# Own tiles for the gate one-hots, and two stage buffers instead of three, in a PEER trunk kernel

## The chip, the cores and the metric

The kernel runs on one core of a Trainium2 chip. A core has four compute engines that run side by side, each with its own instruction queue: TensorE (PE, matrix products), VectorE (DVE), ScalarE (ACT) and GpSimd (POOL). SyncE (SP) only issues transfers; ACT and POOL issue some as well. Engines wait for one another through semaphores. The metric is the device time of one execution in microseconds (us), as the median of several runs.

## The reference

One layer of a decoder trunk over 1024 tokens of width 1024: a mixer with three branches, then an expert network in which each token uses 128 of 16384 experts (8 heads, 16 each).

```python
x = x + hybrid_mixer(rms_norm(x, norm_mix), ...)        # stick-breaking, sparse and recurrent branch
x = x + peer_ffn(rms_norm(x, norm_ffn), w_q, sub_keys, u_tab, v_tab)
return rms_norm(x, norm_final)

# peer_ffn, for 128 tokens at a time
s = einsum("nhad,akd->nhak", (xc @ w_q).reshape(...), sub_keys)   # two sets of 128 keys
top_s, top_i = top_k(s, 16)                                       # then the 16 best of the 256 sums
eidx = first * 128 + second                                       # expert number
gate = softmax(best_s)
hpre = einsum("nd,nhkd->nhk", xc, u_tab[eidx])
act = gate * gelu(hpre)
out = einsum("nhk,nhkd->nd", act, v_tab[eidx])
```

## The kernel before

**Two ways for the experts.** The tokens are worked in four parts of 256 (`PARTS`). For parts 0 and 3 the chosen rows of `u_tab` and `v_tab` are gathered one by one: GpSimd issues an indirect transfer, VectorE multiplies or adds the row (`gather_tile`, L1145 to L1157, tiles `u`, `v`, `gacc`). Parts 1 and 2 (`DENSE`, 512 tokens) go through all 16384 experts: a loop over 128 blocks of 128 experts forms `g = u . h` (`gemm1`, L1386), applies the nonlinearity, multiplies by a gate that is zero for experts not chosen (`gt`, L1429), and sums `g . v` into PSUM (`gemm2`, L1434). This loop comes after the mixer and takes the last 1470 us; it is called the dense loop here. The gathers run beside everything from the first routing on.

**The gates of the dense parts.** The dense loop needs, per token, a 128 x 128 table of gates: row and column are the two halves of the expert number. The 128 choices of a token are scattered into that table by a matrix product of one-hots. `spread_pieces` (L1204) does it four tokens at a time, and a call of `four(q)` is one batch: L1215 compares the two index halves with 0 to 127 (one-hots `hs[:, 0:2]`), L1216 multiplies the second one-hot by the gate's high and low half (`hs[:, 2:4]`), eight matmuls (L1219, L1220) make the four tables in a PSUM tile `gb`, and ScalarE copies them to a staging buffer (L1222). Four batches fill a staging buffer with 16 tokens; then the ACT queue writes it to DRAM (L1224, 1 MB) into `d_G`. There are 128 batches and 32 groups, half of them for part 1 and half for part 2.

**Where these tiles live.** The one-hots are 4 KB per partition and come from the pool `w4` (`W4`, L103), four buffers taken in turn by many users: rows of `x`, norm weights, the routing's own one-hots, and, in the dense loop, the blocks of `u` (`uraw`, L1390). The staging buffers are three: two halves of `stages` (L293) and a tile `stage` of the pool `per`, chosen by `u = n0 // 16 % 3`. `stages` has the tag `h2`: its memory is given to the tile `h2` (L1382), the operand of the dense loop, when the mixer ends. `h2` is loaded from DRAM (`d_hx`, L1384) once the last transfer out of `stages` is done. The last two groups (`n0 >= TH - 32`) go to `stage`, as the group before them does.

**What sets the order.** The program text is written out by a planner (L1305 to L1379) that mixes the pieces of one part with those of others; spread pieces are fillers without a due time. Near the end of the mixer it alternates two spread pieces with one piece of the last part's tail: `merge` (the branch products `pb`, with L919 and L921), then `wo` (output projections `pj_wo`, with weights `w_wo` loaded by SP at L248). Then the framework orders each engine's instructions by priority, over a modelled run in which a tile is taken when a buffer of its pool is free; so the order on an engine may differ from the program's. [...] Projections and `gb` share the two PSUM buffers `ps_mm`.

Of the kernel before, what the change touches and what calls it, by code (L numbers as in the profile page):

```python
# [10 lines left out]
F32 = mybir.dt.float32  # L11
F16 = mybir.dt.float16
# [23 lines left out]
TH = 512  # L36
# [35 lines left out]
def trunk(ctx: ExitStack, tc: tile.TileContext, a: dict, out: bass.AP):  # L72
# [15 lines left out]
    per = mix.enter_context(tc.tile_pool(name="per", bufs=1))  # L88
# [14 lines left out]
    def W4(name, shape=(128, 1024), dt=F32):  # L103
        return w4.tile(list(shape), dt, tag="w4", name=name)
# [188 lines left out]
    stages = hpl.tile([128, 2, 128, 16], F32, tag="h2", name="stages", bufs=1)  # L293
# [910 lines left out]
    def spread_pieces(pt):  # L1204

        stage = {}

        def four(q):
            n0 = pt.t0 - TD + q * 4
            if q % 4 == 0:  # L1210
                u = n0 // 16 % 3 if n0 < TH - 32 else 2
                stage[0] = per.tile([128, 128, 16], F32, tag="stage", name=f"stage{n0}") if u == 2 else stages[:, u]
            sp = spread[pt.i][:, :, q * 4:q * 4 + 4]
            hs = W4(f"hot{n0}", (128, 4, 128, 4), F16)
            V.tensor_tensor(hs[:, 0:2], iorep.unsqueeze(1).to_broadcast([128, 2, 128, 4]), sp[:, 0:2].unsqueeze(2).to_broadcast([128, 2, 128, 4]), op=ALU.is_equal)  # L1215
            V.tensor_tensor(hs[:, 2:4], hs[:, 1:2].to_broadcast([128, 2, 128, 4]), sp[:, 2:4].unsqueeze(2).to_broadcast([128, 2, 128, 4]), op=ALU.mult)  # L1216
            ps = ps_mm.tile([128, 4, 128], F32, tag="mm", name=f"gb{n0}")
            for n in range(4):
                P.matmul(ps[:, n, :], hs[:, 0, :, n], hs[:, 2, :, n], start=True, stop=False)  # L1219
                P.matmul(ps[:, n, :], hs[:, 0, :, n], hs[:, 3, :, n], start=False, stop=True)  # L1220
            m0 = q % 4 * 4
            S.activation(stage[0][:, :, m0:m0 + 4].rearrange("p i n -> p n i"), ps, AF.Copy, scale=SA / SGT)  # L1222
            if q % 4 == 3:
                nc.scalar.dma_start(d_G[n0 // 16], stage[0])  # L1224

        return [lambda q=q: four(q) for q in range(pt.n // 4)]
# [338 lines left out]
```

## Time and profile before

| what | value |
|---|---|
| median of 3 runs | 3559.37 us (3555.66 to 3559.86) |
| the profiled execution | 3556.94 us, its span 3555.1 us |
| clock granted to TensorE, mean | 0.937 |
| L1215, one instruction | 0.683 us (median), 128 of them |
| L1216, one instruction | 0.683 us (median), 128 of them |
| L1222, one copy to a staging buffer | 1.067 us (median), 128 of them |
| first and last L1215 | 1190.5 and 2071.5 us |
| first matmul of the dense loop | 2083.30 us |

Times in the trace count from the start of the span. A row of the timeline gives the start, the length, the engine and line, the operation with output and inputs, and, in brackets, how long the engine stood idle before it and which instruction ended that idle time. `SPq` and `ACTq` are the issues of transfers on those queues. A row of the waits names who waited for whom, then the total, the number of times and the longest.

### The profile page before, as it was taken

What the parts mean: (1) busy time and instruction counts of PE and PEld (TensorE: products, weight loads), DVE (VectorE), ACT (ScalarE), POOL (GpSimd) and SP (SyncE); (2) the same over time, 40 slices, a digit from 0 to 9 for tenths busy, and PEclk for the clock granted to TensorE, in tenths of its full rate; (3) what the DMA queues carried; (4) which work ended last, traced back from release to release, by engine and by line L of the source; (5) the groups of instructions that cost most, each with busy time, mean ns of one, the idle gap of its engine ahead of it and who ended that gap; (6) DMA issues with size and microseconds to landing.
All of it is one profiled execution on the core that took longest, in us unless ns stands there. A gap on an engine that the chain in (4) does not pass through costs nothing.

```text
span 3555.1 us, 57087 instructions
## 1 busy us (share of the span) xinstructions
PE 3255.7 (92%) x20660; PEld 2181.6 (61%) x20660; DVE 3001.0 (84%) x6662; ACT 1599.9 (45%) x3162; POOL 1360.4 (38%) x1166
## 2 busy tenths in 40 slices
PE   7999899999997799999878879869999999999996
PEld 6887777777876587887666644434444444444443
DVE  5665669888789888888998868999988998989898
ACT  5776454653543465644356333234334333333332
POOL 0000001343332242223322234347764765766664
PEclk9999999999997799999778899989999999999998
DMA  8964865989977587897656799789998999999997
GB/s 303 322 240 150 279 206 197 327 314 311 360 284 239 170 307 253 307 331 277 219 190 214 278 353 332 242 267 372 388 375 314 375 381 351 371 352 380 342 373 260
DMA packets 359336, 1058.07 MB, mean 298 GB/s; under 512 B 35238, under 2 KB 107626, under 8 KB 354444
## 3 DMA queue, kind: packets, MB, share of 16 engines
q0 software_dynamic: 147456, 536.94, 42.1%
q1 hardware_dynamic: 206988, 483.93, 38.4%
q10 hardware_dynamic: 4608, 33.56, 2.4%
q8 instruction: 162, 2.65, 0.3%
q14 instruction: 122, 1.00, 0.1%
HBM read 944.19 MB, written 110.10 MB: 297 GB/s over the span
## 4 chain that ended last, share of the span: by engine, by line
PE 53%; DVE 23%; DMA 9%; issue 7%; ACT 6%; POOL 1%; SPq 0%; ACTq 0%; DVEq 0%; POOLq 0%
PE g L258 13%; PE acc L1436 10%; PE pj_mg L258 4%; DVE u L1147 4%; PE g L1436 3%; DVE gacc L1157 3%; PE pj_r_hg L258 2%; DMA v<-in_peer_v_dram,gidx 2%; PE pb L258 2%; DMA gt<-d_G 2%; DMA u<-in_peer_u_dram,gidx 2%; PE pj_wo L258 2%; PE gb L1219 1%; PE gb L1220 1%; PE z_sb L410 1%
## 5 line engine op out<-in xcount | busy, mean ns | idle before, releaser
L1155 POOL DMA_INDIRECT v<-in_peer_v_dram,gidx x421 | 553.6, 1315 | 689.8 <-DVE gacc L1157 410.1
L1145 POOL DMA_INDIRECT u<-in_peer_u_dram,gidx x417 | 523.5, 1255 | 636.8 <-DVE u L1147 404.9
L258 PE MATMUL g<-h,us 128*128 128x512 f16 x3072 | 690.8, 382 | 17.1 <-DVE ts L982 6.2
L1157 DVE SCALAR_TENSOR_TENSOR gacc<-v,act,gacc 128x1024 f32<-128x1024 f32 x421 | 538.1, 1278 | 35.4 <-DMA v<-in_peer_v_dram,gidx 31.8
L1436 PE MATMUL acc<-vs,ac 128*128 128x512 f16 x2304 | 536.8, 381 | 20.6 <-ACT vs L213 7.8
L1436 PEld LDWEIGHTS <-ac 128*128 128x128 f16 x3072 | 302.0, 98 | 411.4 <-issue 50.1
L258 PEld LDWEIGHTS <-us 128*128 128x128 f16 x3072 | 302.0, 98 | 385.1 <-issue 17.8
L1147 DVE SCALAR_TENSOR_TENSOR u<-u,gh 128x1024 f32<-128x1024 f32 x417 | 501.8, 1216 | 34.3 <-DMA u<-in_peer_u_dram,gidx 33.8
L1395 ACT ACTIVATE ge<-g 128x512 f32<-128x512 f32 x128 | 76.2, 595 | 528.7 <-PE g L258 498.4
L258 PE MATMUL pj_mg<-hT,w_mg 128*128 128x256 f16 x2304 | 273.9, 274 | 6.3 <-ACT mg L881 3.9
L258 PEld LDWEIGHTS <-w_mg 128*128 128x128 f16 x2304 | 226.8, 100 | 37.6 <-issue 11.8
L1436 PE MATMUL g<-vs,ac 128*128 128x512 f16 x768 | 184.0, 383 | 23.6 <-ACT ge L1395 23.6
L214 DVE SCALAR_TENSOR_TENSOR vs<-vraw,vs 128x1024 f16<-128x1024 f32 x128 | 154.8, 1215 | 25.9 <-ACT vs L213 25.8
L1145 POOL DMA_INDIRECT rr_u<-in_peer_u_dram,gidx x95 | 137.1, 1444 | 89.5 <-DVE rr_u L1147 66.3
L213 ACT ACTIVATE vs<-vraw 128x1024 f16<-128x1024 f32 x128 | 132.6, 1046 | 84.8 <-DMA vraw<-in_peer_v_dram 84.8
L213 ACT ACTIVATE ac<-ge 128x512 f16<-128x512 f32 x128 | 80.0, 628 | 200.7 <-DVE ge L1429 161.3
L1155 POOL DMA_INDIRECT rr_v<-in_peer_v_dram,gidx x90 | 130.7, 1453 | 94.3 <-DVE gacc L1157 71.5
L214 DVE SCALAR_TENSOR_TENSOR us<-uraw,us 128x1024 f16<-128x1024 f32 x128 | 155.6, 1215 | 9.8 <-ACT us L213 9.1
L258 PE MATMUL pb<-o,w_b 128*128 128x256 f16 x1152 | 144.8, 282 | 20.3 <-DVE sg L919 16.7
L1219 PE MATMUL gb<-hot 128*128 128x128 f16 x512 | 126.1, 294 | 39.2 <-DVE hot L1216 21.2
L258 PE MATMUL pj_r_hg<-hT,w_r_hg 128*128 128x256 f16 x1152 | 143.5, 283 | 7.1 <-ACT iv_hg L739 4.7
L1429 DVE TENSOR_TENSOR ge<-ge,gt 128x256 f32<-128x256 f32 x256 | 97.9, 419 | 55.7 <-ACT ge L1395 30.2
(1141 smaller groups left out, 6422.0 us busy)
## 6 DMA issues: line engine op xcount, KB each, us to landing
uraw<-in_peer_uT_dram SPq DMA_DIRECT2D x128, 512.0 KB, 7.2
vraw<-in_peer_v_dram SPq DMA_DIRECT2D x128, 512.0 KB, 8.1
w_mg<-dw SPq DMA_DIRECT2D x72, 512.0 KB, 5.0
gt<-d_G SPq DMA_DIRECT2D x32, 1024.0 KB, 18.5
d_G<-stages ACTq DMA_DIRECT2D x20, 1024.0 KB, 5.2
w_r_hg<-dw SPq DMA_DIRECT2D x36, 512.0 KB, 5.2
w_b<-dw SPq DMA_DIRECT2D x72, 256.0 KB, 5.0
wr_mg<-in_wblk_dram SPq DMA_DIRECT2D x24, 512.0 KB, 4.9
```

Source lines behind the costliest of these rows:

```text
L213: S.activation(hi, src, AF.Copy, scale=scale)
L214: V.scalar_tensor_tensor(lo, in0=src, scalar=scale, in1=hi, op0=ALU.mult, op1=ALU.subtract)
L258: P.matmul(ps, l[:, k, :], r[:, k, :], start=(i == 0), stop=(i == n - 1))
L410: P.matmul(x["z"], st["q"][b:b + 64, tl * 128:(tl + 1) * 128], st["k"][b:b + 64, r0 + c0:r0 + c1], start=True, stop=(c0 > 0))
L1145: G.indirect_dma_start(out=ur, out_offset=None, in_=a["peer_u"], in_offset=bass.IndirectOffsetOnAxis(ap=idx[:, c:c + 1], axis=0))
L1147: V.scalar_tensor_tensor(ur, in0=ur, scalar=1.0, in1=h2, op0=ALU.mult, op1=ALU.mult, accum_out=hpre[:, c:c + 1])
L1155: G.indirect_dma_start(out=vr, out_offset=None, in_=a["peer_v"], in_offset=bass.IndirectOffsetOnAxis(ap=idx[:, c:c + 1], axis=0))
L1157: V.scalar_tensor_tensor(acc, in0=vr, scalar=act[:, c:c + 1], in1=acc, op0=ALU.mult, op1=ALU.add)
L1219: P.matmul(ps[:, n, :], hs[:, 0, :, n], hs[:, 2, :, n], start=True, stop=False)
L1395: S.activation(ge, ps, AF.Gelu, scale=1.0 / (SW * SH2))
L1429: V.tensor_tensor(gv, gv, gt[:, :, i % 8, :], op=ALU.mult)
L1436: P.matmul(ps, ac[:, x, t * 128:(t + 1) * 128], v[:, y, dh * 512:(dh + 1) * 512], start=start and n == 0, stop=stop and n == 2)
```

## The change

The one-hots get a tag of their own with two buffers in the pool `per`, and leave `w4`. The tile `stage` goes; all 32 groups take turns in the two halves of `stages`, the last two included. The memory is the same: 8 KB per partition for `stage` before, two times 4 KB for `hot` now.

```diff
             if q % 4 == 0:
-                u = n0 // 16 % 3 if n0 < TH - 32 else 2
-                stage[0] = per.tile([128, 128, 16], F32, tag="stage", name=f"stage{n0}") if u == 2 else stages[:, u]
+                stage[0] = stages[:, n0 // 16 % 2]
             sp = spread[pt.i][:, :, q * 4:q * 4 + 4]
-            hs = W4(f"hot{n0}", (128, 4, 128, 4), F16)
+            hs = per.tile([128, 4, 128, 4], F16, tag="hot", name=f"hot{n0}", bufs=2)
```

## The prediction

> **What bounds the kernel now.** I read the page first (busy time, then the chain that ended last), then busy time by stretch, then the hand-over from the mixer to the dense expert loop row by row.
>
> ```profile
> span 3555.1 us, 57087 instructions
> PE 3255.7 (92%) x20660; PEld 2181.6 (61%) x20660; DVE 3001.0 (84%) x6662; ACT 1599.9 (45%) x3162; POOL 1360.4 (38%) x1166
> ...
> PE 53%; DVE 23%; DMA 9%; issue 7%; ACT 6%; POOL 1%; SPq 0%; ACTq 0%; DVEq 0%; POOLq 0%
> ```
>
> TensorE carries 53% of the chain and VectorE 23%, so a microsecond counts where PE stands idle. By stretch (start:end, length, then busy time and instructions of PE, PEld, DVE, ACT, POOL, then clock, DMA share, GB/s):
>
> ```profile
> 1790.00:2083.00 293.00, 235.57 (x1591) 189.07 (x1591) 244.60 (x438) 156.77 (x271) 85.97 (x73) 0.81 0.70 243
> 2083.00:2500.00 417.00, 367.54 (x1789) 181.30 (x1790) 376.80 (x879) 137.68 (x188) 200.65 (x145) 0.94 0.89 315
> 2500.00:3000.00 500.00, 500.00 (x2319) 226.66 (x2317) 458.42 (x590) 173.02 (x229) 313.35 (x224) 1.00 0.98 362
> ```
>
> Up to 2083 PE idles 293.00 - 235.57 = 57 us in 293, and from 2500 to 3000 not at all. So a hand-over that comes earlier moves a full PE queue earlier, and should show at the end. The change acts between 1190 and 2118, where one-hots and gate groups are made and first read. A batch below is four tokens (one call of `four`), a group four batches.
>
> **Part 1: one-hots in two tiles instead of a share of four.** Nothing is computed differently: 128 batches, each with one L1215 and one L1216. The shared pool let up to four batches stand between VectorE and TensorE. With two, the L1215 of a batch waits for the matmuls of the batch two before it; so far it waited for one four before.
>
> ```profile
> L1215 DVE TENSOR_TENSOR hot<-iorep,spread x128: 665/683/751, 1190.5 to 2071.5; 128x1024 f16<-128x1024 f16 x128
> ...
> DVE hot L1215 <- PE gb L1220: 27.6, 34, 4.1
> ```
>
> I matched the 128 L1215 with the 1024 gb matmuls in order. Of the 126 batches that have one two before them, 109 began before that one's matmuls ended. The first (third batch, second of the x2) and the last:
>
> ```profile
> 1191.73 1.28 DVE L1215 TENSOR_TENSOR hot<-iorep,spread 128x1024 f16<-128x1024 f16 x2
> ...
> 1212.77 0.28 PE L1219 MATMUL gb<-hot 128*128 128x128 f16 x1
> ...
> 2071.48 0.69 DVE L1215 TENSOR_TENSOR hot<-iorep,spread 128x1024 f16<-128x1024 f16 x1 [0.25 <-PE gb L1220]
> ...
> 2075.72 0.30 PE L1219 MATMUL gb<-hot 128*128 128x128 f16 x1
> ```
>
> The third began some 20 us before the first batch's matmuls were even issued; the last began 4 us before the start of the last L1219 of the batch two before. All 109 have to move back. Does TensorE notice? A batch's two VectorE operations need about 1.4 us (twice 0.683 from the row). From the end of one batch's matmuls to the start of the matmuls two batches later there was more than that nearly everywhere, mostly 2 to 20 us, because projections lie between; summed over all batches only 1.2 us were missing. So if L1215 merely moves back in VectorE's order, the price is near 1.2 us. I take **+2 us**. The low end is 0; the high end is the slow rival's +14. What is queued behind a waiting L1215 on VectorE: gather products (L1147, L1157), whose rows release GpSimd's next gathers; the branch products L919, which release PSUM for the next pb matmuls; and the scans that `sb` logits wait for.
>
> **Part 2: groups in two buffers.** Three groups in turn become two. Mostly this costs nothing: a group's write takes 5.2 us (median, row below), and the group between lasts longer (the 28th group's write goes out at 2048.36, the 29th's at 2055.40, counted from 0). The cover ends only if a write takes over 7 us. What it removes is at the end, where groups 29, 30 and 31 all go through the one `stage`:
>
> ```profile
> 2048.36 0.33 ACTq L1224 DMA_DIRECT2D d_G<-stages  x1
> ...
> 2055.40 0.35 ACTq L1224 DMA_DIRECT2D d_G<-stage  x1
> ...
> 2068.29 1.95 ACT L1222 ACTIVATE stage<-gb 128x512 f32<-128x512 f32 x2 [10.62 <-DMA d_G<-stage]
> ...
> 2077.45 1.96 ACT L1222 ACTIVATE stage<-gb 128x512 f32<-128x512 f32 x2 [2.07 <-DMA d_G<-stage]
> ...
> 2081.74 0.33 ACTq L1224 DMA_DIRECT2D d_G<-stage  x1
> ```
> ```profile
> 2069.39 0.28 PE L1219 MATMUL gb<-hot 128*128 128x128 f16 x1 [10.26 <-ACT stage L1222]
> ...
> 2078.56 0.28 PE L1219 MATMUL gb<-hot 128*128 128x128 f16 x1 [1.72 <-ACT stage L1222]
> ...
> 2083.30 1.03 PE L258 MATMUL g<-h,us 128*128 128x512 f16 x2 [2.69 <-ACT us L213]
> ```
> ```profile
> 2055.40 12.81 DMA d_G<-stage
> ...
> 2096.21 20.54 DMA gt<-d_G
> ```
>
> TensorE lost 10.26 + 1.72 = **12.0 us** to a buffer not yet written out. After the change group 30 waits for 28 (landed by about 2053.6) and group 31 for 29 (2055.40 + 5.2 = 2060.6, while group 30 is still made). Both waits go, and the last write, at 2081.74, goes out near 2081.7 - 12.0 = 2069.8.
>
> **What is late next.** `stages` and the loop's operand `h2` share one buffer. Until now groups 30 and 31 stayed out of it, so the SP queue could load h beside them:
>
> ```profile
> 2037.84 0.95 SPq L100 DMA_DIRECT2D gf<-in_norm_ffn_dram  x1
> 2039.39 0.32 SPq L248 DMA_DIRECT2D w_wo<-dw  x1
> 2055.10 0.80 SPq L100 DMA_DIRECT2D h<-d_hx  x2
> 2075.93 16.29 SPq L100 DMA_DIRECT2D uraw<-in_peer_uT_dram  x7
> 2092.26 0.42 SPq L248 DMA_DIRECT2D w_wo<-dw  x1
> ...
> 2095.74 11.98 SPq L1424 DMA_DIRECT2D gt<-d_G  x2
> ```
> ```profile
> d_G<-stages ACTq DMA_DIRECT2D x20, 1024.0 KB, 5.2
> ```
> ```profile
> DMA to landing us min/median/max: 5.7/5.7/5.7
> ```
>
> The last of these rows is the h load's. It now waits for the last write: 2069.8 + 5.2 + 5.7 = 2080.7. The first g started at 2083.30, so of the 12.0 us only **2.6** remain. This assumes the first uraw loads are no longer last: they waited for one-hots to leave the pool (first issue 2075.93) and now find its four tiles free. SP does not keep program order (gf, needed after all of w_wo, is issued at 2037.84, before w_wo loads at 2092.26), so I take them as issued ahead of h; the two operations of `us` then also lie before 2080.7. If they stay behind h, the 2.6 us are gone. If the last write takes the 12.81 us of the one at 2055.40, g starts at 2088.3, 5.0 late; that is my bad end. The good end is 12.0, if projections fill TensorE's wait.
>
> **Behind the first g.** The gate tiles gt were issued at 2095.74, behind the uraw loads that waited, and 20.54 us later the first product could run. TensorE was not full there:
>
> ```profile
> 2055.00:2069.00 14.00, 4.13 (x37) 3.72 (x35) 9.23 (x13) 1.47 (x3) 6.75 (x4) 0.77 0.92 343
> 2069.00:2083.00 14.00, 9.29 (x72) 8.11 (x71) 9.80 (x10) 8.41 (x10) 6.65 (x6) 0.74 0.83 289
> 2083.00:2105.80 22.80, 22.27 (x97) 9.65 (x98) 14.21 (x12) 7.44 (x9) 7.43 (x7) 0.93 1.02 404
> 2105.80:2118.00 12.20, 8.71 (x54) 5.00 (x53) 5.90 (x14) 3.50 (x5) 0.00 (x0) 1.00 1.14 327
> ```
> ```profile
> 2414.13 5.18 PE g L258 x24
> ```
>
> The last stretch holds 12.20 - 8.71 = 3.5 us of idle. With 2 MB of uraw out of the way gt can go out near 2076 and land near 2097, while four blocks of g (5.18 us each) keep TensorE busy to 2080.7 + 20.7 = 2101. I take all **3.5 us**; the ends are 0 and 3.5.
>
> The clock column stands at 0.77 and 0.74 in the two idle stretches. [...]
>
> **Sum.** -2.6 - 3.5 + 2.0 = -4.1 us. Against the profiled execution (3556.94 us, span 3555.1) that is 3552.8; that execution lies 2.4 us under the median of the three runs, 3559.37, so I forecast 3559.4 - 4.1 = **3555 us**.
>
> **Rivals.** *Slower: two one-hot tiles stall VectorE.* Place: 1190 to 2083, in front of L1215. Today 34 waits cost 27.6 us, 0.81 each. If the 109 batches all pay that, it is 88 us, 61 more; at VectorE's 23% of the chain +14 us. The balance is -2.6 - 3.5 + 14 = +8: 3567 us. It decides from 6.1/0.23 = 27 us of extra idle before L1215. For it: VectorE is 83% busy in 1790 to 2083, so what waits there is not easily made up. Against it: the 1.2 us of missing slack. [...] Chance 0.24.
>
> *Much faster: the wait for h is filled.* Between the last gb and 2080.7 TensorE has no g, but output projections of the last part are due:
>
> ```profile
> 2106.72 2.78 PE L258 MATMUL pj_wo<-m,w_wo 128*128 128x256 f16 x24 [0.57 <-DVE x L937]
> ```
>
> With four of them (2.78 us each) moved in, the whole 12.0 stay: -12.0 - 3.5 + 2.0 = -13.5, 3546 us. Against it: in the idle of 2059 to 2069 none was moved in, their weights coming through the SP queue behind h and uraw. Chance 0.34.
>
> *Nothing reaches the end.* The last chain is VectorE's gather sums, not TensorE:
>
> ```profile
> 3529.93 1.29 DVE gacc L1157
> ```
>
> If GpSimd's gathers keep their pace, an earlier dense loop only waits for them: 3559 us, chance 0.06. The forecast keeps 0.36.
>
> **How the numbers follow.** About 0.2% (7.1 us) is what a measurement of this kernel can tell from no change. The forecast's own range is 3550 to 3562, from -9.6 (3.5 and half of the 12.0) to +2.5. Faster by over 0.2%: 0.34 and 0.03 of the forecast's chance, 0.37; slower 0.24; within 0.39. The range takes in -13.5 with some 6 us below it and the slow rival's +8 with the late h load (5.0) on top: 3540 to 3573.
>
> **What would show it.** Right: no idle on PE before gb from `stage`; h issued right after the last write landed; the first uraw issued long before; the first g near 2081; less idle between the first g and the first acc. Slow rival: idle before L1215 well over 55 us, and the last gb later than 2080. Fast rival: pj_wo between the last gb and the first g. Wrong altogether: a new order of the queues before 1790 that moves the hand-over by more than 10 us, which no row here can price.

## The result, and the profile after

The change made the kernel slower, and the forecast was wrong on the sign.

| kernel | median | profiled execution | its span |
|---|---|---|---|
| before | 3559.61 us (3548.85 to 3567.55, 6 runs) | 3556.94 us | 3555.1 us |
| after | 3586.93 us (3575.03 to 3598.45, 6 runs) | 3579.61 us | 3577.8 us |

The ratio is 1.0086, 95% interval 1.0064 to 1.0107: some 30 us (the medians differ by 27), outside the forecast range of 3540 to 3573. In the new kernel the names of the lines are one lower (L1214 and L1215 are the one-hots, L1223 is the write of a group).

The gf load of SyncE (L100, the one at 2037.84 before) goes out two to three microseconds behind the fifth-last group's write in both kernels, and is the mark from which I count. In the profiled execution of after it lies at 2030.23 (start of the first stretch below), 7.6 us earlier than before. Since runs of one kernel spread over some 20 us, I read nothing into that, and compare distances from gf.

The transfers that SyncE issues at the hand-over in after (start, length, line, output and input; neighbours of one kind are drawn together, with the time between them):

```profile
2042.40 27.74 SPq L100 DMA_DIRECT2D uraw<-in_peer_uT_dram  x4
2074.93 0.33 SPq L100 DMA_DIRECT2D vraw<-in_peer_v_dram  x1
2075.31 0.43 SPq L1423 DMA_DIRECT2D gt<-d_G  x1
2075.79 12.21 SPq L100 DMA_DIRECT2D vraw<-in_peer_v_dram  x2
2088.11 2.00 SPq L100 DMA_DIRECT2D h<-d_hx  x2
2090.16 11.54 SPq L1423 DMA_DIRECT2D gt<-d_G  x2
```

The uraw loads did go ahead, as assumed. But h, which before went out at 2055.10, now stands behind three vraw loads and a gt load. The 12.21 us of the two vraw loads are nearly all one issue, the one right behind gt; below it the view of the tile vraw, all 128 issues with minimum, median and maximum in ns:

```profile
2075.79 11.74 SPq L100 DMA_DIRECT2D vraw<-in_peer_v_dram  x1
```
```profile
L100 SPq DMA_DIRECT2D vraw<-in_peer_v_dram x128: 327/328/11736, 2074.9 to 3543.0; - x128
```

In this stretch the waits of SyncE name no engine and no transfer that would account for it (one wait of 1.5 us for TensorE is all): the issue itself took 11.74 us where 0.33 is usual. The group writes of the ACT queue, and what TensorE did meanwhile:

```profile
2041.23 0.33 ACTq L1223 DMA_DIRECT2D d_G<-stages  x1
2052.69 0.33 ACTq L1223 DMA_DIRECT2D d_G<-stages  x1
2063.73 0.33 ACTq L1223 DMA_DIRECT2D d_G<-stages  x1
2076.01 0.33 ACTq L1223 DMA_DIRECT2D d_G<-stages  x1
```
```profile
2074.61 0.29 PE L1219 MATMUL gb<-hot 128*128 128x128 f16 x1
2101.88 13.23 PE L258 MATMUL g<-h,us 128*128 128x512 f16 x48 [26.98 <-DMA h<-d_hx]
2119.95 7.54 PE L258 MATMUL g<-h,us 128*128 128x512 f16 x24 [4.84 <-ACT ge L1394]
2127.33 0.38 PE L1435 MATMUL acc<-vs,ac 128*128 128x512 f16 x1
```

No wait for a staging buffer is left. In its place stands one wait of 26.98 us, for h. From the last write to the issue of h it is 2088.11 - 2076.01 = 12.1 us, from there to the first g 13.8 us: in those 13.8 us (2088.11 to 2101.88) the DMA share was 1.07 at 376 GB/s, an estimated 5.2 MB, and h is 2 MB of them: vraw and gt loads, issued just ahead of h and behind it, were under way too.

Where the time went shows in three stretches counted from gf (0 to 46, 46 to 80, 80 to 400 us; the columns are those of the prediction's table of stretches). First before, then after:

```profile
2037.84:2083.84 46.00, 29.70 (x242) 26.19 (x241) 33.99 (x48) 18.87 (x23) 17.25 (x14) 0.84 0.89 322
2083.84:2117.84 34.00, 30.41 (x148) 14.48 (x146) 19.40 (x26) 10.52 (x13) 7.27 (x6) 0.96 1.06 377
2117.84:2437.84 320.00, 274.43 (x1353) 138.53 (x1354) 294.68 (x752) 107.07 (x148) 147.48 (x109) 0.93 0.85 295
```
```profile
2030.23:2076.23 46.00, 33.10 (x240) 27.22 (x239) 40.45 (x57) 21.36 (x25) 15.31 (x13) 0.82 0.87 310
2076.23:2110.23 34.00, 8.35 (x27) 3.24 (x28) 13.39 (x11) 3.17 (x3) 9.52 (x8) 0.54 1.04 353
2110.23:2430.23 320.00, 273.50 (x1363) 139.13 (x1362) 276.44 (x725) 103.47 (x144) 123.95 (x99) 0.93 0.78 270
```

TensorE lost 30.41 - 8.35 = 22.1 us of work in the middle stretch alone; the other two differ by +3.4 and -0.9. Counted in matmuls (the x of the first column), after is at 1630 when before is at 1743, 400 us behind gf. At 5.18 us for 24 matmuls of the dense loop (the prediction's row at 2414.13), the 113 missing ones are an estimated 24 us. Far behind, TensorE is full in both kernels (busy for 500.00 of the 500 us from 2500 to 3000); the 65th gelu of the dense loop (ge, one for each block of 128 experts), before and after:

```profile
2840.65 0.60 ACT L1395 ACTIVATE ge<-g 128x512 f32<-128x512 f32 x1 [5.36 <-PE g L258]
```
```profile
2858.38 0.60 ACT L1394 ACTIVATE ge<-g 128x512 f32<-128x512 f32 x1 [6.95 <-PE g L258]
```

From gf it is 802.8 us before and 828.2 after, +25.3. From there to the end of the span it is 714.5 and 719.4, +5. So of the profiled span's +22.7, -7.6 lie ahead of gf, **+25.3 between gf and the 65th gelu**, where the hand-over lies, and +5.0 behind.

### The profile page after: what moved, and what is told of

It is laid out like the page before. It is cut to its first block, busy times and chain, and to the rows that moved or that the text cites. A ratio compares the mean times of both kernels' runs of the same rounds, so it can differ in the third digit from the quotient of the medians.

```text
span 3577.8 us, 57087 instructions
## 1 busy us (share of the span) xinstructions
PE 3262.0 (91%) x20660; PEld 2183.9 (61%) x20660; DVE 3006.2 (84%) x6662; ACT 1600.1 (45%) x3164; POOL 1358.4 (38%) x1166
## 3 DMA queue, kind: packets, MB, share of 16 engines
q8 instruction: 162, 2.65, 0.3%
## 4 chain that ended last, share of the span: by engine, by line
PE 52%; DVE 23%; DMA 9%; issue 7%; ACT 7%; POOL 2%; SPq 0%; DVEq 0%; POOLq 0%; ACTq 0%
PE g L258 12%; PE acc L1435 9%; DVE gacc L1157 5%; PE pj_mg L258 4%; PE g L1435 3%; DMA u<-in_peer_u_dram,gidx 3%; DMA vraw<-in_peer_v_dram 2%; DVE u L1147 2%; PE pj_r_hg L258 2%; PE pb L258 2%; PE pj_wo L258 2%; DMA v<-in_peer_v_dram,gidx 2%; POOL u L1145 1%; PE z_sb L410 1%; PE gb L1218 1%
## 5 line engine op out<-in xcount | busy, mean ns | idle before, releaser
L1157 DVE SCALAR_TENSOR_TENSOR gacc<-v,act,gacc 128x1024 f32<-128x1024 f32 x421 | 542.0, 1287 | 34.8 <-DMA v<-in_peer_v_dram,gidx 30.8
L1435 PE MATMUL g<-vs,ac 128*128 128x512 f16 x768 | 185.2, 383 | 14.1 <-ACT ge L1394 11.1
L1221 ACT ACTIVATE stages<-gb 128x512 f32<-128x512 f32 x128 | 134.2, 1064 | 101.0 <-PE gb L1219 95.1
```

The lines of the kernel that those rows point to most:

```text
L1157: V.scalar_tensor_tensor(acc, in0=vr, scalar=act[:, c:c + 1], in1=acc, op0=ALU.mult, op1=ALU.add)
L1435: P.matmul(ps, ac[:, x, t * 128:(t + 1) * 128], v[:, y, dh * 512:(dh + 1) * 512], start=start and n == 0, stop=stop and n == 2)
```

## The experiments

My theory from here on ("h"): the loss is the late load of h. The first rival ("depth"): it is the two-deep one-hots. A second: it is the changed order of other loads on SyncE's queue. All ratios are to the kernel before, run beside them on the same chip.

| kernel | ratio, 95% interval | idle of TensorE before the first g, and what ended it | first g after gf |
|---|---|---|---|
| before | 1 | 2.69, us | 45.5 |
| after | 1.0086 (1.0064 to 1.0107) | 26.98, h | 71.7 |
| stage_only | 1.0067 (1.0044 to 1.0091) | 39.89, h | 72.8 |
| shift | 0.9998 (0.9982 to 1.0013) | 2.65, us | 44.6 |
| h_first | 1.0048 (1.0030 to 1.0066) | 20.18, h | 62.6 |
| depth4_h_first | 1.0064 (1.0044 to 1.0085) | 25.35, h | 58.2 |
| before_late_h | 1.0100 (1.0083 to 1.0118) | 38.48, h | 73.4 |
| w4_tail | 1.0003 (0.9988 to 1.0018) | 22.25, us | 61.1 |
| depth4_w4_tail | 1.0051 (1.0034 to 1.0067) | 4.01, us | 47.8 |
| before_w4 | 1.0032 (1.0018 to 1.0046) | 3.16, us | 46.2 |
| after_at | 1.0021 (1.0000 to 1.0041) | 0.21, the copy of a tail | 46.3 |
| before_at | 1.0006 (0.9989 to 1.0022) | 9.31, us | 40.6 |
| at_hot4 | 1.0025 (1.0008 to 1.0041) | 18.67, us | 49.9 |
| at_hot1 | 1.0129 (1.0102 to 1.0155) | none | 52.9 |
| gt_late | 1.0123 (1.0094 to 1.0152) | 25.46, h | 68.5 |

**Parts alone.** stage_only is the change with its first part undone: the one-hots back in `w4`, groups in two halves. shift is the kernel before with the turns moved by one, so that groups 28, 30 and 31 use `stage` and one of the two waits for it should go.

```diff
-            hs = per.tile([128, 4, 128, 4], F16, tag="hot", name=f"hot{n0}", bufs=2)
+            hs = W4(f"hot{n0}", (128, 4, 128, 4), F16)
```
```diff
-                u = n0 // 16 % 3 if n0 < TH - 32 else 2
+                u = (n0 // 16 + 1) % 3 if n0 < TH - 32 else 2
```

> Only the second part of the change: one-hots stay in the shared pool of four, the groups take turns in the two halves of stages, the last two too. Theory H (the hand-over: h shares the memory of stages, so its load now waits for the last write of a group, and behind other loads on SP): still slow, ratio to before 1.004 to 1.010, first g some 15 to 30 us later than before's 2083, PE idle over 15 us in front of it for h. Theory D (depth: two one-hot tiles stall VectorE and TensorE): as fast as before or faster, ratio 0.996 to 1.001, for the 12 us of idle before gb for the one stage are gone and nothing else changed.

> The kernel before, with the turn of its three buffers moved by one, so that group 29 goes to stages and 28, 30 and 31 to stage. h still waits for no later write than that of group 29. The two waits of ACT for the one stage (10.6 and 2.1 us) become one. If these waits delay the loop (both theories say so), the first g comes 5 to 10 us sooner than 2083, ratio 0.997 to 0.999; if the hand-over is bound by something else, no change, 0.999 to 1.001.

The last group writes of stage_only, and what TensorE waited for there:

```profile
2033.69 0.33 ACTq L1223 DMA_DIRECT2D d_G<-stages  x1
2042.38 0.33 ACTq L1223 DMA_DIRECT2D d_G<-stages  x1
2049.55 0.33 ACTq L1223 DMA_DIRECT2D d_G<-stages  x1
2056.73 0.33 ACTq L1223 DMA_DIRECT2D d_G<-stages  x1
```
```profile
PE g L258 <- DMA h<-d_hx: 39.9, 1, 39.9
```

From the write of group 28 to that of group 31 it takes 23.0 us, where it took 33.4 before and 34.8 in after. So two buffers in place of three do save some 10 us at the mixer's end while the one-hots stay four deep; with two-deep one-hots the saving is gone. But the saving is of no use either way: h goes out 25.2 us after the last write, behind gt, vraw and uraw loads (2081.90), so it comes no earlier, and TensorE just waits longer for it. And the kernel is slow (1.0067) although its one-hots are four deep; "depth" had asked for 0.996 to 1.001 here. In shift a wait of 11.3 us for `stage` was left, and nothing was gained. The first part alone (own one-hots beside three staging buffers) wasn't tried; it needs 8 KB more per partition than either kernel.

**h ahead of vraw and gt.** h_first is the change with the vraw and gt loads held behind h on SyncE's queue; in depth4_h_first, besides, pairs of batches alternate between the two own tiles and `w4`, so that one-hots are four deep.

```diff
+        h_load = nc.cur_bb.bb.instructions[-1]     # behind load(h2[:, j], d_hx[j])
-        raw = load(late.tile([128, D], F32, tag="vraw", ...), ...)
+        vr = late.tile([128, D], F32, tag="vraw", ...)
+        with tc.issue_after(h_load):
+            raw = load(vr, ...)
+                with tc.issue_after(h_load):
                     nc.sync.dma_start(gt, ...)
```
```diff
-            hs = per.tile([128, 4, 128, 4], F16, tag="hot", name=f"hot{n0}", bufs=2)
+            hs = per.tile([128, 4, 128, 4], F16, tag="hot", name=f"hot{n0}", bufs=2) if n0 // 8 % 2 else W4(f"hot{n0}", (128, 4, 128, 4), F16)
```

> The changed kernel, with the loop's loads of v and of the gates told to stand behind the load of h on SP. Nothing else differs. Theory H: the load of h goes out as soon as the last group is written (near 2081 instead of 2088) and lands sooner with less beside it, the first g near 2088 instead of 2102; about 12 us less, ratio 1.004 to 1.006. Theory D: the loop starts earlier but the time lost to one-hots between 1190 and 2075 stays; under 5 us less, ratio 1.007 or more.

> As h_first, and the one-hots have four tiles in turn again (two of their own and two from the shared pool, in pairs). Theory D: another 8 to 15 us less than h_first, ratio 0.999 to 1.002, idle before L1214 back to some 28 us and the last gb 8 to 14 us sooner after the load of the norm weights (gf at 2030 in the changed kernel). Theory H: depth costs nothing, the same as h_first within 4 us.

SyncE's queue in h_first and in depth4_h_first:

```profile
2091.44 0.80 SPq L100 DMA_DIRECT2D h<-d_hx  x2
```
```profile
2049.56 21.74 SPq L100 DMA_DIRECT2D uraw<-in_peer_uT_dram  x8
2071.39 0.87 SPq L100 DMA_DIRECT2D h<-d_hx  x2
...
2072.90 17.88 SPq L1427 DMA_DIRECT2D gt<-d_G  x2
```

In h_first h goes out 7.8 us after the last write (2083.62) and needs another 11 to the first g; about half of the loss goes (1.0048). A part of what is left is built in: h can't be loaded before the last group is out. In depth4_h_first the last write is at 2063.09, yet h lands only at about 2086.9, with uraw ahead of it and 2 MB of gt behind it. It is no faster than h_first (1.0064 against 1.0048, intervals that overlap): "depth" had asked for 0.999 to 1.002. The order on the queue is a part of the loss, not the whole.

**What holds h on the queue: gt or the vraw buffers?** There are only two vraw buffers, so the third vraw load ahead of h might have held the queue as well. gt_late is h_first without its vraw part: gt alone is held behind h, and four vraw loads stay ahead of it.

> The changed kernel with only the gt loads held behind h on SyncE's queue; the first four vraw loads stay ahead of h. In the changed kernel the vraw load right behind the first gt took 11.74 us to issue, with no wait on another engine in the trace, where a vraw issue takes 0.33. If gt holds whatever is issued behind it: here the first two vraw issues take 0.33 us each, the third and fourth wait, if at all, visibly for VectorE's or ScalarE's work on the vraw buffers, and the gt issues behind h are long instead. If it was the vraw buffers: a long vraw issue is there without gt in front. Time: h about 8 to 13 us behind the last write, as in h_first or a little later, 1.004 to 1.008.

Its queue, issue by issue, and SyncE's waits from 2080 to 2097 (total, times, longest):

```profile
2081.39 0.33 SPq L100 DMA_DIRECT2D vraw<-in_peer_v_dram  x1
2081.77 0.42 SPq L100 DMA_DIRECT2D vraw<-in_peer_v_dram  x1
2092.17 0.33 SPq L100 DMA_DIRECT2D vraw<-in_peer_v_dram  x1
2096.16 0.33 SPq L100 DMA_DIRECT2D vraw<-in_peer_v_dram  x1
2096.59 0.37 SPq L100 DMA_DIRECT2D h<-d_hx  x1
...
2097.49 0.62 SPq L1425 DMA_DIRECT2D gt<-d_G  x1
2098.16 10.75 SPq L1425 DMA_DIRECT2D gt<-d_G  x1
```
```profile
SPq L100 <- DMA vraw<-in_peer_v_dram: 8.9, 2, 7.6
SPq L100 <- DVE vs L214: 4.7, 2, 2.4
```

Without gt in front a vraw issue takes 0.33 us again, and the long issue has moved behind the first gt (10.75). So gt holds what is issued behind it. The whole trace of before says the same: 33 issues of SyncE took over 2 us there, and 32 of them stand right behind a gt load. But h gained nothing: now the vraw buffers hold it, with waits that the trace does name (8.9 and 4.7 us), and it goes out 14.1 us after the last write (2082.47), against 12.1 in after. So either can hold h: gt did in after, the vraw buffers do here. The forecast missed twice, on h (8 to 13 us behind the last write) and on the time (1.004 to 1.008, measured 1.0123). Whether it is slower than after is not shown, since the intervals overlap; its first g comes no later.

**The wait for h by itself.** before_late_h is the kernel before with one choice of buffer changed: the last group goes to a half of `stages`, whose memory h needs. Four-deep one-hots and three buffers stay. w4_tail is the opposite: the whole change, but the last two groups are staged in two tiles of `w4` each, out of h's memory.

```diff
-                u = n0 // 16 % 3 if n0 < TH - 32 else 2
+                u = n0 // 16 % 3 if n0 < TH - 32 else (1 if n0 >= TH - 16 else 2)
```
```diff
                 stage[0] = stages[:, n0 // 16 % 2]
+                if n0 >= TH - 32:
+                    stage.update({z: W4(f"tail{n0}_{z}", (128, 64, 16)) for z in range(2)})
...
+            if n0 >= TH - 32:
+                for z in range(2):
+                    S.activation(stage[z][:, :, m0:m0 + 4].rearrange("p i n -> p n i"), ps[:, :, z * 64:z * 64 + 64], AF.Copy, scale=SA / SGT)
+                    if q % 4 == 3:
+                        nc.scalar.dma_start(d_G[n0 // 16][:, z * 64:z * 64 + 64, :], stage[z])
+                return
```

> The kernel before, only the last group goes to a half of stages, so that h waits for the last write; one-hots as before, three buffers as before. Theory 'h': idle of 15 to 30 us before the first g, first g 55 to 70 us after gf, 1.004 to 1.008. Theory 'depth': 1.000 to 1.002.

> The changed kernel, but the last two groups are staged in the pool w4 (two tiles of 4 KB each, so two copies and two half writes a group), and nothing of them lies in the memory of h. Theory 'h': h can go out about 17 us after the load of gf, as before; the 27 us of idle before the first g go; the first g starts 47 to 50 us after gf (before 45.5, changed kernel 71.6), the first acc about 82 (80.1, 97.1); the time comes back to 0.999 to 1.003 of before. Theory 'depth' (the two-deep one-hots are the loss): the one-hots are as in the change, so 1.006 to 1.010 whatever h does. Mixed: h is worth about half, 1.003 to 1.006.

SyncE and TensorE in before_late_h, then in w4_tail:

```profile
2077.00 17.42 SPq L100 DMA_DIRECT2D vraw<-in_peer_v_dram  x1
...
2097.06 1.88 SPq L100 DMA_DIRECT2D h<-d_hx  x2
```
```profile
2114.39 12.05 PE L258 MATMUL g<-h,us 128*128 128x512 f16 x48 [38.48 <-DMA h<-d_hx]
```
```profile
2065.23 0.81 SPq L100 DMA_DIRECT2D h<-d_hx  x2
```
```profile
2099.67 1.03 PE L258 MATMUL g<-h,us 128*128 128x512 f16 x2 [22.25 <-ACT us L213]
```

This is the cleanest pair. One changed choice of buffer in the kernel before makes it as slow as the change (1.0100, more than I had forecast), through the same chain: h behind a vraw load whose issue, right behind gt, takes 17.42 us. And the change with h's memory left free is within 0.2% of before (1.0003), though its one-hots are two deep: the depth rival asked for 1.006 to 1.010 here and for 1.000 to 1.002 in before_late_h, and falls at both. My own forecast of the first g in w4_tail (47 to 50 us after gf) missed too: uraw goes out only at 2089.53, behind a vraw issue of 11.10 us that stands right behind gt, and TensorE waits 22.25 us for `us`. That uraw went there because the tail tiles fill `w4` is likely, not shown. This idle costs little: the first acc comes 79.1 us after gf, as before (80.1), against 97.1 in after, and 400 us after gf TensorE is 42 matmuls behind before, where after is 113 behind. Why it is made up is open.

**Is there anything to win?** before_w4 is shift with group 31 staged in `w4`; depth4_w4_tail is w4_tail with four-deep one-hots. after_at and before_at do as w4_tail and before_w4, but stage the tail in four tiles a group of the attention's pool `at`, which neither h nor uraw uses (after_at also holds the 5th to 8th uraw load behind h).

```diff
+                if n0 >= TH - 32:                 # before_at: n0 >= TH - 16
+                    stage.update({z: W2(f"tail{n0}_{z}") for z in range(4)})
```

> The kernel before with its turns shifted by one (so that groups 30 and 28 use stage) and group 31 staged in w4: no group waits for a buffer and h goes out early. If the 12.0 us that TensorE lost to the one stage are worth their size, as the prediction had it: last write 32 to 36 us after gf, first g 36 to 42 (45.5 before), 0.997 to 0.999. If a wait for us or h stands behind them anyway: 1.000.

> As w4_tail, and the one-hots alternate in pairs of batches between their own two tiles and two of w4, so four deep. Both theories: first g 36 to 45 us after gf. Theory 'h': depth is worth at most 10 us at the hand-over; 0.997 to 1.001. Theory 'depth': this one comes back to 1.000 and w4_tail does not. If both are slow (1.005 or more), the loss lies in neither, but in what else moved (the orders of the queues).

> The changed kernel (one-hots two deep, 29 groups and the first in the two halves) with the last two groups staged in the pool 'at' of the attention (eight tiles of 2 KB, four copies and four quarter writes a group), which neither h nor uraw needs; the 5th to 8th uraw load held behind h on the SP queue. Theory 'h': h goes out 17 to 28 us after gf, uraw is there, no idle over 5 us before the first g, which starts 45 to 52 us after gf (two-deep one-hots still cost their 10 us); 0.997 to 1.001. Theory 'depth': 1.004 or more.

> The kernel before, turns shifted by one and group 31 staged in four tiles of the pool 'at': one-hots four deep, no wait for a staging buffer, h and uraw early. Last write 32 to 36 us after gf (43.9 before), first g 36 to 42 (45.5). If the 12.0 us of the one stage are worth their size: 0.996 to 0.998. If a later wait (vraw and gt, which need the mixer's memory and the last write) takes their place: 0.999 to 1.001.

before_at does what part 2 of the change was thought to do, without its price: no wait for a staging buffer, four-deep one-hots, h and uraw early. TensorE there:

```profile
2077.04 1.03 PE L258 MATMUL g<-h,us 128*128 128x512 f16 x2 [9.31 <-ACT us L213]
2078.83 22.53 PE L258 MATMUL g<-h,us 128*128 128x512 f16 x94 [0.76 <-DVE us L214]
...
2106.55 9.63 PE L1445 MATMUL acc<-vs,ac 128*128 128x512 f16 x36 [4.97 <-ACT ac L213]
```
```profile
2036.47:2082.47 46.00, 33.38 (x251) 27.15 (x251) 35.75 (x50) 20.94 (x36) 18.66 (x13) 0.86 0.91 348
2082.47:2116.47 34.00, 29.03 (x129) 12.91 (x128) 18.96 (x25) 11.12 (x15) 9.28 (x7) 0.94 1.08 373
2116.47:2436.47 320.00, 268.46 (x1338) 136.41 (x1336) 287.35 (x738) 101.74 (x142) 134.71 (x107) 0.92 0.83 285
```

The first g comes 40.6 us after gf, 4.9 earlier than before, and TensorE is 2.3 us ahead in the first 80 us; in the next 320 us it falls 6.0 behind. The ratio is 1.0006 (12 us less would be 0.9966, outside its interval): the 12.0 us of the one `stage` are worth nothing at the end in this form. after_at has no gap at all before the first g and gains nothing either (1.0021, between its two forecasts). before_w4 and depth4_w4_tail miss their forecasts, and they are slow (1.0032 and 1.0051) although their first g comes within 2.4 us of before's: a late h is not the only way to lose time here. In both, one-hots, tail and uraw compete for the four tiles of `w4`; in depth4_w4_tail TensorE waited 11.5 us for one-hots and 13.5 us for `us`. That this competition makes the loss is argued, not shown. No version beat the kernel before.

**Depth by itself.** at_hot4 and at_hot1 are after_at with the one-hots in `w4` (four deep), and with `bufs=1`.

> As after_at, but the one-hots back in w4 (four deep): only part 1 of the change undone, h early. From gf to the last write 34 to 38 us (after_at 53). If two-deep one-hots cost end to end what they cost at the mixer's end (about 10 us): 0.3% below after_at, that is 0.998 to 1.000 of before; if that is hidden by what follows: the same as after_at, 1.001 to 1.003.

> As after_at, but the one-hots one deep: the suspected cost of part 1 doubled or more, since each one-hot then waits for the batch just before. If depth costs end to end: 1.005 to 1.015 and idle before L1216 of 100 us or more in place of 52; if it is hidden: 1.002 to 1.004.

The writes of groups 28 and 29 of at_hot1:

```profile
2107.15 0.33 ACTq L1231 DMA_DIRECT2D d_G<-stages  x1
2121.68 0.33 ACTq L1231 DMA_DIRECT2D d_G<-stages  x1
```

Between these two groups it is 14.5 us with one tile, 11.5 with two (after, 2041.23 to 2052.69), and 8.7 with four (stage_only, 2033.69 to 2042.38). So depth does set the pace of a mixer's end that nothing else holds up. One tile instead of two costs some 1.1% (1.0129 against 1.0021), and earlier than that: gf goes out 50.3 us later than in after_at. TensorE waited 88.0 us for one-hots, 18.6 in after_at. The sign that I had named for it, idle of VectorE before the one-hots of 100 us, did not come: it was 58.9, for 52.1 in after_at. Between two tiles and four no difference can be told in the time: 1.0021 and 1.0025. at_hot4 is no clean answer, though: its last quarter write (2074.70) goes out 48.5 us after gf, not 34 to 38 as forecast. The first uraw load goes out at 2054.30, but ScalarE takes up `us` only at 2075.07, right behind that write, and TensorE waits 18.67 us for it. What two-deep one-hots would cost where both had room stays open.

## Why the prediction was wrong

**Late h: the step that failed.** The prediction put the first g at "2069.8 + 5.2 + 5.7 = 2080.7": h goes out when the last write lands, and takes 5.7 us (the landing of one load of 1 MB, the only one that the trace of before gives; h is two of them). Counted from gf that is 42.9 us; it took 71.7. Half of the miss (15.0 us) is this step itself: 25.9 us from the last write to the first g instead of 10.9. I had moved h behind the last write without asking what else would then stand ahead of it on SyncE's queue. Next to it I counted it as a gain that gt "can go out near 2076". It did (2075.31), with vraw, ahead of h. The two terms were summed as if they were independent, and they share one queue, and were under way together (DMA share 1.07 from the issue of h to the first g). That a gt load holds the queue stood in the trace of before, and in the prediction's own row of two gt issues (2095.74, 11.98 us), whose second is

```profile
2096.21 11.51 SPq L1424 DMA_DIRECT2D gt<-d_G  x1
```

Each of the 32 issues right behind a gt load took from 2.45 to 15.68 us in before. Even the bad end, 2088.3, let only the write be slow. before_late_h shows that a late h alone can make a loss of this size.

**Part 1, "+2": wrongly sized, and in the trace of after this is the other half of the miss.** The slack of 1.2 us was measured in an order of events in which `stage` held up the last groups. With that wait gone, two-deep one-hots are the next limit: groups 28 to 31 took 34.8 us where the prediction's step needs 33.4 - 12.0 = 21.4, and stage_only took 23.0. The last write came 45.8 us after gf, not 2069.8 - 2037.84 = 32.0. TensorE's waits from 2030 to 2080 name the one-hots, which in before it did not wait for between gf and the first g; below it VectorE's idle before the one-hots in the whole span:

```profile
PE gb L1218 <- DVE hot L1215: 9.4, 5, 3.8
```
```profile
DVE hot L1214 <- PE gb L1219: 39.9, 38, 4.0
```

The latter is 39.9 us for 27.6 before. But the two halves don't add: with the one-hots four deep (stage_only) the last write comes 34.1 us after gf, and the first g as late as in after, 72.8. In the end time this term can't be seen (w4_tail, after_at, at_hot4).

**Part 2, 12.0 us off TensorE.** Both waits went, as said. In before_at, without them, the 12 us did not arrive at the end, so that "only 2.6 remain" was right in kind: something stands behind them.

**Behind the first g, -3.5.** From the first g to the first acc it was 34.7 us and is 25.5 now, but that is because the first g is late. TensorE's idle between the two, which the term was to remove, rose from 3.7 us to 4.8.

**Rivals.** The slow rival had the sign right and the mechanism wrong: its first sign, idle before the one-hots well over 55 us, failed (39.9). Its second, a last gb later than 2080, is met only when counted from gf: the last gb, at 2074.61, lies 44.4 us behind it, which would be 2082.2 in before. The fast rival didn't happen: no pj_wo stands between the last gb and the first g. "Nothing reaches the end" is refuted for a delay: the 25.3 us lost by the 65th gelu arrive at the end (span +22.7). Whether a gain would arrive is not shown: in before_at TensorE had lost its lead again by 400 us after gf.

**Right.** The first uraw loads went out long before the first g, and h's wait for the last write was seen as the thing that eats the gain; its size was not.

## What to carry to other kernels

When two tiles share memory, ask which load inherits the wait and where it stands on its queue: what was behind it may pass it and then hold it up. Don't sum terms that use one queue as if each had it alone, look in the old trace for what that neighbour does to the issues behind it, and don't measure the slack for a shallower buffer in a schedule that the same change speeds up. A buffer whose only purpose seems to be avoiding a wait may be there to keep another tile's memory free.

## What the runs showed of the hardware

The gt loads held SyncE's queue. The issue right behind the first gt load (1 MB) took 11.74 us in after, 17.42 in before_late_h and 10.75 in gt_late; the median vraw issue in after took 0.33. Why a gt load does this, no run here shows.

TensorE's clock after the long wait. In after, the stretch of the wait for h (columns as in the tables of stretches):

```profile
2075.00:2102.00 27.00, 0.12 (x1) 0.12 (x2) 12.36 (x11) 4.16 (x5) 7.91 (x7) 0.50 1.01 353
```

The granted clock stands at 0.50. It stayed there for the first 5.50 us of work (2101.88 to 2107.38), and 13 g began in them; in the 7.73 us from 2107.38 to 2115.11 it was 1.00, and the other 35 began. All 48 g took 13.23 us, where twice the 5.18 us of 24 g at a granted clock of 1.00 (before, 2414.13 to 2419.31) make 10.36: 2.9 us on top of the idle. Half of the 5.50 us, an estimated 2.75, accounts for nearly all of it. In before_late_h the first 48 took 12.05 us, 1.7 on top.

The landing of h. One of its two loads of 1 MB took 5.7 us to land in before, with a DMA share of 0.81 (2055.10 to 2060.80). In after TensorE's wait for h ended 13.8 us after the first of them was issued, with gt and vraw under way beside them and a DMA share of 1.07.
